# First step of the recurrence's query and forget products in float32, 512-column products in some blocks, and other orders, in a two-layer hybrid block on one Trainium2 core

## The chip, the cores and the metric

The kernel runs on one core of a Trainium2 chip. The metric is the device time of one execution in microseconds; lower is better. In what follows PE is the TensorE matmul unit, PEld its weight load, DVE is VectorE, ACT is ScalarE, POOL is GpSimd, and SP is the SyncE queue that issues most transfers.

## What is computed

The input `x` has 256 tokens of width 1024, one batch, two layers. Shift, scale and gate rows are linear in `silu(c)`, four sets and one for the shared keys and values. Cut to what matters:

```python
h = modulate(x, norm_mix[0], shift, scale)          # layer 0: a gated linear recurrence
q, f, i, g = split(h @ w_in)                        # each 256 x 1024
q = silu(q); log_f = log_sigmoid(f); k = -expm1(log_f)
# per head, chunks of 64 tokens: o = (q * exp(G)) @ state + masked, decayed (q k) @ i
o = rms_norm(o, out_norm) * silu(g)
x = x + gate * (o @ w_out)
x = x + gate * swiglu(modulate(x, ...), ffn_w_in[0], ffn_w_out[0])   # hidden width 2816
kv = modulate(x, kv_norm, ...) @ w_kv               # shared keys, values: compressed, selected, window
q, gates = modulate(x, norm_mix[1], ...) @ w_q      # layer 1: attention, 16 heads of 64, 3 branches
x = x + gate * (attention(q, kv, gates) @ w_out)
x = x + gate * swiglu(modulate(x, ...), ffn_w_in[1], ffn_w_out[1])
```

All inputs and outputs are float32.

## The kernel before

**Products.** Activations lie transposed, feature on the partition, 8 chunks of 128 features by 256 tokens. A float32 product is made of three faster products of split operands: weights are split into `wh` (a rounded copy, type fp32r, made by ACT) and `wl` (the rest, made by DVE), activations into `hh` and `hl`. `mm3` (lines 533 to 537) does `wh·hh`, `wh·hl`, `wl·hh`, 256 columns each. `gemm_wide` (539 to 548) does the first two as one product of 512 columns over `hh` and `hl`, into two halves of a PSUM tile that are added afterwards, and the third with 256 columns. Before, the wide form runs in both second products of the feed-forward layers (`ffo`, from `g`), and in the first product of layer 1 from block 3 on (`WIDE = (1,)`). Small attention products take float32 operands directly, and each shows as two instructions in the trace.

**Weights.** All weights are one list of 1 MB pieces, `SCHED`, in the order in which they are used. SP loads them in that order into a ring of four buffers (`raw`, line 298); a piece is loaded when the piece four before it is no longer read. `process` (302 to 338) takes the next piece: a `lin` piece is split in two halves, `wh` by ACT (line 321) and `wl` by DVE (line 325); an `ada_ss` or `ada_g` piece is reduced against `silu(c)` by two DVE operations (line 390); `pe_ss` and `pe_g` pieces, for four of the sets, go through PE as 32-column float32 products (line 429). The two late pieces of `w1`, for the compressed keys, are loaded into the tile `h0` (`load_late`, line 360).

**Order.** The program is written down in one order, and a planner orders each engine's instructions before the run, by this order, by what is ready and by priorities (`PRI`; a positive number moves earlier, a negative later). At run time each engine works through its list strictly in order. `ORDER` is the order of the recurrence's steps (`hgrn`), of the attention's steps (`nsa`), and the places of the shift, scale and gate pieces in the lists of three stages (`hada`, `f0`, `f1`): a number is the place in the main list before which a piece is put.

**Start.** `startup` and `first_stat` compute the norm of `x`. The recurrence's `q` and `f` (8 steps `hg_qf`, one per 128 features, 16 output tiles in eight PSUM tiles) alternate with the 8 pieces of scale and shift rows of the first set. `first_product` (line 611) does step 0 by hand: the split of its weights in three parts, `t` (L630), `hh` (L631), `hl` (L633), with the order on ACT and DVE written out by `chain`. `first_chunk` makes `hh` and `hl` of the later steps (L745 to L750).

**Tiles.** `h_tiles` gives the activations of two alternating sets: set 0 is one tile `h0` with `hh` and `hl` side by side per chunk, set 1 two tiles `hh1` and `hl1`. The same two tiles hold scratch at the start (`sqs`, `xr0`) and in the recurrence (`s0`, `s1`).

**Attention.** `nsa` computes shared keys and values from the un-normalised `h` where it can (`gemm_deferred`), then two normalised sets by `full_pair`: `hq` for queries and `hk` for values. The masks `QACT` and `KACT` say for which of the 8 chunks ACT makes `t`; DVE makes the others. `hk` takes the tile `h0`, which the late pieces of `w1` hold until the compression has read them. The output projection `nsa_out` runs with `gemm` over `self.O`, and `residual` adds into `x` (L800) and makes the next `hh`, `hl` (L586, L587).

Of the kernel before, what the change touches and what calls it, by code (L numbers as in the profile page):

```python
# [11 lines left out]
F32 = mybir.dt.float32  # L12
F32R = mybir.dt.float32r
# [3 lines left out]
AF = mybir.ActivationFunctionType  # L17
ALU = mybir.AluOpType
# [3 lines left out]
P = 128  # L22
S = 256
D = 1024
KD = 8
FH = 2816
NF = FH // P
CH = 2048
# [4 lines left out]
WIDE = (1,)  # L33
ROOTED = [("ffn_in0", 2, 1), ("ffn_in0", 3, 0), ("kv", 2, 0), ("kv", 4, 0), ("ffn_in1", 2, 1), ("ffn_in1", 3, 0)]
PTS = 3
QACT, KACT = 0x0F, 0xF0
CSTK = 7

PRI = {"gates": -100, "av": 10, "res": 60, "rot": -15, "fh": 60}
# [16 lines left out]
def _ada_g(l):  # L56
# [9 lines left out]
        "D0 k i0 +g0 +i1 +g1 S0/4 x c0 c1 D1 i2 +i3 V0 +g2 +T0 S1/4 +g3 x G0 V1 T1 o0 H o1 G1 o2 o3"  # L66
    ).split(),
    "hada": [1, 1, 2, 2, 3, 3, 4, 4, 7, 7, 8, 8],
    "f0": [7, 7, 8, 8, 9, 13, 15, 16, 16, 16, 21, 21, 22, 23, 25, 26, 28, 29, 31, 32],
    "nsa": (  # L70
        "K q0 c0 c1 G w0 q1 R n0 x0 q3 w1 s0 s1 s2 q2 v0 v1 n1 a s3 a s4 v2 a v3 a x1 s5 s6 v4 v6 s7 a a a a v5 a v7 a a a"
    ).split(),
    "f1": [15, 16, 24, 29],
# [126 lines left out]
class K:  # L200
# [364 lines left out]
    def h_tiles(self, which):  # L565
        if which == 0:

            self.h0 = self.hp.tile([P, KD, 2, 258], F32R, tag="h0", name="h0")
            return self.h0[:, :, 0], self.h0[:, :, 1]
        hh = self.hp.tile([P, KD, 258], F32R, tag=f"hh{which}", name=f"hh{which}")  # L570
        hl = self.hp.tile([P, KD, 258], F32R, tag=f"hl{which}", name=f"hl{which}")
        return hh, hl
# [38 lines left out]
    def first_product(self, hh, hl, pool):  # L611
# [5 lines left out]
        ws = [[self.wp.tile([P, CH // 2], F32R, tag=n, name=f"{n}1_{h}") for n in ("wh", "wl")] for h in range(2)]  # L617
        parts = [(0, 0, 2), (0, 2, 8), (1, 0, 8)]

        def hi(h, a, b):  # L620
            return nc.scalar.copy(ws[h][0][:, a * P:b * P], u[:, h * D + a * P:h * D + b * P])

        def lo(h, a, b):
            s = slice(a * P, b * P)
            return nc.vector.tensor_tensor(ws[h][1][:, s], u[:, h * D + a * P:h * D + b * P],
                                           ws[h][0][:, s].bitcast(F32), op=ALU.subtract)

        t = pool.tile([P, 2, S], F32, tag="X", bufs=XBUFS, name="t0")[:, 0]
        his = [hi(*parts[0])]
        ts = nc.vector.scalar_tensor_tensor(t, self.x[:, 0], A[:, 0:1], self.rstd, op0=ALU.mult, op1=ALU.mult)  # L630
        h = nc.scalar.activation(hh[:, 0, :256], t, AF.Identity, bias=sh[:, 0:1])  # L631
        los = [lo(*parts[0])]
        hls = nc.vector.scalar_tensor_tensor(hl[:, 0, :256], t, sh[:, 0:1], hh[:, 0, :256].bitcast(F32),  # L633
                                             op0=ALU.add, op1=ALU.subtract)
        for p in parts[1:]:
            his.append(hi(*p))
            los.append(lo(*p))
        self.chain(*on_act[:-1], his[0], on_act[-1], h, *his[1:])
        self.chain(on_dve[-1], ts, los[0], hls, los[1], los[2])
        self.hl_prev = los[2]  # L640
        self.issue(self.n_proc + RAW)
        return ws
# [5 lines left out]
    def startup(self, crow):  # L648
# [3 lines left out]
        sq = self.hp.tile([P, KD * 258], F32, tag="hh1", name="sqs")[:, :KD * S].rearrange("p (k s) -> p k s", k=KD)  # L652
# [42 lines left out]
    def first_stat(self):  # L695
# [15 lines left out]
        self.xr0 = self.hp.tile([P, KD * 258], F32, tag="hl1", name="xr0")[:, :KD * S].rearrange("p (k s) -> p k s", k=KD)  # L711
# [108 lines left out]
    def hgrn(self):  # L820
# [3 lines left out]
        with self.tc.tile_pool(name="hg", bufs=1) as gp, self.tc.tile_pool(name="hg2", bufs=2) as g2:  # L824
# [4 lines left out]
            for k in range(KD):  # L829
# [10 lines left out]
                for h, w in enumerate(self.fetch("hg_qf", k, ahead=0) if k else self.first_product(hh, hl, g2)):  # L840
# [7 lines left out]
            s0 = self.hp.tile([P, KD * 258], F32, tag="hh1", name="s0")  # L848
# [893 lines left out]
```

## Time and profile before

| | us |
|---|---|
| three runs | 723.38, 720.93, 723.20 |
| median | 723.2 |
| profiled execution, device time | 723.27 |
| its span, first to last instruction | 721.5 |

| engine or path | what the page says |
|---|---|
| granted PE clock, mean | 0.998 |
| HBM read | 170.48 MB, 238 GB/s over the span |
| `raw` pieces of 1024 KB | 153 issues on SP, median 5.5 us to landing |
| `ffo` products (L547, 512 columns) | 330, 116.0 us busy |
| `ff` products (L535, L536, L537, 256 columns) | 352 each, 98.9 to 99.1 us busy |
| reductions on DVE (L390) | 64, 77.9 us busy |

Matmuls are pipelined: a 256-column split product shows some 0.28 us from start to end, while the next one starts about 0.12 us after it. So busy us of PE summed by line exceed the time that passes. A row of the page gives line, engine, operation, output and inputs, shapes and count, then busy us and mean ns of one, then the engine's idle time just before these instructions and what ended it.

### The profile page before, as it was taken

The page shows a single profiled execution, that of the slowest core. Times are in us where ns is not written, and L with a number is a line of the kernel's source. Part 1 is how long each engine was busy: PE and PEld are TensorE (multiplying, and loading weights), DVE is VectorE, ACT ScalarE, POOL GpSimd, SP SyncE. Part 2 cuts the span into 40 slices and gives each one's busy share as a digit, 9 for nine tenths or more (in the row PEclk, how much of TensorE's full clock was granted, in tenths as well). Part 3 has the DMA queues.
Part 4 walks back from the last instruction along what each step waited for, and adds up shares of the span by engine and source line. Part 5 has one row for each costly group of instructions (what it writes and reads, how often), then busy time and mean ns, then how long its engine had stood idle before and what let it go on. Part 6 is the DMA issues. An engine that isn't in the chain of part 4 may idle for free.

```text
span 721.5 us, 14615 instructions
## 1 busy us (share of the span) xinstructions
PE 710.4 (98%) x5843; PEld 628.2 (87%) x5843; DVE 578.9 (80%) x1177; ACT 418.5 (58%) x825; POOL 12.3 (2%) x29
## 2 busy tenths in 40 slices
PE   8999999999999999999999999999999999999998
PEld 5999788899999999988898896555999888888887
DVE  6997896589998989889598798878779878776651
ACT  5659877567636454544376555559657656564430
POOL 0000000000000000000002020100000000000000
PEclk9999999999999999999999999999999999999999
DMA  9899865734599898888548542674445757556720
GB/s 356 334 367 381 334 255 194 269 126 175 179 343 369 315 347 341 318 304 341 198 148 289 207 151 70 248 281 187 176 175 177 256 204 258 202 197 232 241 81 23
DMA packets 27926, 174.05 MB, mean 241 GB/s; under 512 B 3281, under 2 KB 4689, under 8 KB 8018
## 3 DMA queue, kind: packets, MB, share of 16 engines
q1 hardware_dynamic: 26656, 170.80, 64.3%
q0 software_dynamic: 768, 1.57, 0.8%
q8 instruction: 46, 0.75, 0.4%
q10 hardware_dynamic: 434, 0.74, 0.3%
q14 instruction: 22, 0.18, 0.1%
HBM read 170.48 MB, written 1.05 MB: 238 GB/s over the span
## 4 chain that ended last, share of the span: by engine, by line
PE 80%; DVE 7%; ACT 6%; DMA 4%; issue 2%; SPq 0%; ACTq 0%; DVEq 0%
PE ffo L547 11%; PE ff L535 7%; PE ff L537 7%; PE ff L536 6%; PE ffo L548 5%; PE ff L547 5%; DMA raw<-in_w 3%; PE ff L548 2%; PE po L1616 2%; PE adapsss L429 2%; DVE wl L325 2%; ACT wh L321 2%; PE ptt L1598 2%; PE s L1558 2%; ACT Pt L469 1%
## 5 line engine op out<-in xcount | busy, mean ns | idle before, releaser
L321 ACT CAST wh<-raw 128x1024 fp32r<-128x1024 f32 x199 | 206.8, 1049 | 164.0 <-PE ffo L547 43.8
L325 DVE TENSOR_TENSOR wl<-raw,wh 128x1024 fp32r<-128x1024 f32 x199 | 241.2, 1220 | 71.0 <-ACT wh L321 70.9
L547 PE MATMUL ffo<-g,wh 128*128 128x512 f32 x330 | 116.0, 394 | 0.0
L536 PE MATMUL ff<-hl,wh 128*128 128x256 f32 (+1 forms) x352 | 99.1, 282 | 0.0
L537 PE MATMUL ff<-hh,wl 128*128 128x256 f32 (+1 forms) x352 | 99.1, 282 | 0.0
L535 PE MATMUL ff<-hh,wh 128*128 128x256 f32 (+1 forms) x352 | 98.9, 282 | 0.0
L548 PE MATMUL ffo<-g,wl 128*128 128x256 f32 x330 | 93.0, 282 | 0.0
L390 DVE CUSTOM_DVE_ANT_0 junk<-raw,crep 128x1024 f32<-128x1024 f32 x64 | 77.9, 1217 | 3.1 <-DMA raw<-in_w 3.1
L547 PEld LDWEIGHTS ffo<-g,wh 128*128 128x128 f32 x330 | 62.0, 188 | 14.5
L535 PEld LDWEIGHTS ff<-hh,wh 128*128 128x128 f32 x352 | 66.3, 189 | 0.3 <-ACT hh L586 0.2
L537 PEld LDWEIGHTS ff<-hh,wl 128*128 128x128 f32 x352 | 66.5, 189 | 0.0
L536 PEld LDWEIGHTS ff<-hl,wh 128*128 128x128 f32 x352 | 66.4, 189 | 0.0
L548 PEld LDWEIGHTS ffo<-g,wl 128*128 128x128 f32 x330 | 62.0, 188 | 0.0
L547 PE MATMUL ff<-h,wh 128*128 128x512 f32 x152 | 54.1, 394 | 0.0
L548 PE MATMUL ff<-h,wl 128*128 128x256 f32 x152 | 42.6, 281 | 0.0
L469 ACT ACTIVATE Pt<-Pt,nm 128x128 f32<-128x128 f32 x64 | 28.1, 441 | 16.9 <-DVE nm L1567 16.9
L547 PEld LDWEIGHTS ff<-h,wh 128*128 128x128 f32 x152 | 28.7, 189 | 6.6
L548 PEld LDWEIGHTS ff<-h,wl 128*128 128x128 f32 x152 | 28.7, 189 | 0.0
L800 DVE SCALAR_TENSOR_TENSOR x<-ffo,mod,x 128x256 f32<-128x256 f32 x31 | 14.9, 481 | 16.5 <-PE ffo L548 11.5
L530 ACT CAST g<-fg 128x256 fp32r<-128x256 f32 x44 | 17.8, 404 | 17.4 <-DVE fg L1206 16.3
L1563 DVE CUSTOM_DVE_ANT_0 Pt<-s,cst 128x128 f32<-128x128 f32 (+1 forms) x64 | 18.9, 352 | 2.1 <-PE s L1558 2.0
L1042 DVE TENSOR_TENSOR rf<-rf 128x512 f32<-128x512 f32 x28 | 18.3, 685 | 2.2 <-ACT X L1039 1.0
(497 smaller groups left out, 1755.3 us busy)
## 6 DMA issues: line engine op xcount, KB each, us to landing
raw<-in_w SPq DMA_DIRECT2D x153, 1024.0 KB, 5.5
raw<-in_w SPq DMA_DIRECT2D x11, 512.0 KB, 6.9
w1late<-in_w SPq DMA_DIRECT2D x2, 1024.0 KB, 8.7
x<-in_x SPq DMA_DIRECT2D x2, 512.0 KB, 4.7
usq<-huq POOLq DMA_DIRECT2D x16, 64.0 KB, 2.9
out<-x SPq DMA_DIRECT2D x8, 128.0 KB, 1.9
cst<-in_cst ACTq DMA_DIRECT2D x1, 558.0 KB
usk<-huk POOLq DMA_DIRECT2D x8, 64.0 KB, 5.8
```

What stands on the lines that cost most here:

```text
L321: r = nc.scalar.copy(wh, u)
L325: r = nc.vector.tensor_tensor(wl, u, wh.bitcast(F32), op=ALU.subtract)
L390: r = nc.vector.tensor_tensor_reduce(out=junk, in0=t[:, h * D:(h + 1) * D], in1=self.crep, scale=1.0, scalar=0.0, op0=ALU.mult, op1=ALU.ad ...
L469: r = nc.scalar.activation(out, in_, func, **kw)
L530: self.nc.scalar.copy(hi, v)
L535: mm(ps, lhsT=wh, rhs=hh, start=first, stop=False)
L536: mm(ps, lhsT=wh, rhs=hl, start=False, stop=False)
L537: return mm(ps, lhsT=wl, rhs=hh, start=False, stop=last)
L547: mm(ps, lhsT=w[k][0], rhs=b, start=k == 0, stop=False)
L548: mm(ps[:, 0], lhsT=w[k][1], rhs=b[:, 0], start=False, stop=k == n - 1)
L1042: nc.vector.tensor_tensor(fr, fr, ap(rf, 2 * W, [1, 2], [2, n], [0, b]), op=ALU.mult)
L1563: nc.vector.tensor_tensor_reduce(out=Pt[half][:, br, o:o + n], in0=ps[half][:, br], in1=cs[:, S - n:], scale=1.0, scalar=-3e38, op0=ALU.ad ...
```

## The change

Step 0 of `q` and `f` is no longer split: 16 float32 products run from the loaded weight piece and the float32 activation, for which DVE adds the shift (`tf`). `hh` and `hl` of chunk 0 are still made, for the later products with `h`. Set 1 of the activations becomes one tile `h1`, with all of `hh` before all of `hl`, and so do the scratch tiles in its place. Seven blocks of layer 0's first feed-forward product and the attention's output projection take the wide form; the projection's residual then adds two halves. Orders, places and three masks change.

```diff
-WIDE = (1,)
+WIDE = ((4, 11, 14, 16, 17, 18, 21), range(NF))
-QACT, KACT = 0x0F, 0xF0
+QACT, KACT = 89, 241
+PTV = 1
-PRI = {"gates": -100, "av": 10, "res": 60, "rot": -15, "fh": 60}
+PRI = {'gates': -80, 'av': 10, 'res': 50, 'rot': 0, 'fh': 130}
...
     "hgrn": (
-        "D0 k i0 +g0 +i1 +g1 S0/4 x c0 c1 D1 i2 +i3 V0 +g2 +T0 S1/4 +g3 x G0 V1 T1 o0 H o1 G1 o2 o3"
+        "i0 k +i1 +g0 D0 +g1 S0/4 c0 x i2 c1 V0 +g2 +i3 +T0 D1 S1/4 +g3 x H G0 V1 o0 T1 G1 o1 o2 o3"
...
-    "hada": [1, 1, 2, 2, 3, 3, 4, 4, 7, 7, 8, 8],
-    "f0": [7, 7, 8, 8, 9, 13, 15, 16, 16, 16, 21, 21, 22, 23, 25, 26, 28, 29, 31, 32],
+    "hada": [1, 1, 1, 2, 3, 3, 4, 6, 7, 7, 9, 9],
+    "f0": [5, 6, 7, 8, 9, 10, 12, 13, 15, 19, 20, 20, 22, 23, 26, 26, 26, 27, 30, 32],
     "nsa": (
-        "K q0 c0 c1 G w0 q1 R n0 x0 q3 w1 s0 s1 s2 q2 v0 v1 n1 a s3 a s4 v2 a v3 a x1 s5 s6 v4 v6 s7 a a a a v5 a v7 a a a"
+        "q0 K c1 c0 G w0 q1 R n0 q3 q2 x0 s0 w1 s1 s2 v0 v1 n1 s3 s4 v2 a a v3 a a x1 s5 a s6 v4 v6 s7 v5 a a v7 a a a a a"
...
-    "f1": [15, 16, 24, 29],
+    "f1": [10, 20, 21, 32],
...
-        hh = self.hp.tile([P, KD, 258], F32R, tag=f"hh{which}", name=f"hh{which}")
-        hl = self.hp.tile([P, KD, 258], F32R, tag=f"hl{which}", name=f"hl{which}")
-        return hh, hl
+        self.h1 = self.hp.tile([P, 2, KD, 258], F32R, tag="h1", name="h1").rearrange("p e k s -> p k e s")
+        return self.h1[:, :, 0], self.h1[:, :, 1]
...
-    def first_product(self, hh, hl, pool):
+    def first_product(self, hh, hl, pool, out):
...
-        ws = [[self.wp.tile([P, CH // 2], F32R, tag=n, name=f"{n}1_{h}") for n in ("wh", "wl")] for h in range(2)]
-        parts = [(0, 0, 2), (0, 2, 8), (1, 0, 8)]
...
-        self.chain(*on_act[:-1], his[0], on_act[-1], h, *his[1:])
-        self.chain(on_dve[-1], ts, los[0], hls, los[1], los[2])
-        self.hl_prev = los[2]
+        t = pool.tile([P, 2, S], F32, tag="X", bufs=XBUFS, name="t0")
+        ts = nc.vector.scalar_tensor_tensor(t[:, 0], self.x[:, 0], A[:, 0:1], self.rstd, op0=ALU.mult, op1=ALU.mult)
+        tf = nc.vector.tensor_scalar_add(t[:, 1], t[:, 0], sh[:, 0:1])
+        for h in range(2):
+            for m in range(8):
+                nc.tensor.matmul(out[h][m // 2][:, m % 2], lhsT=u[:, h * D + m * P:h * D + m * P + P], rhs=t[:, 1],
+                                 start=m % 2 == 0, stop=False)
+        self.last_hh = nc.scalar.copy(hh[:, 0, :256], t[:, 1])
+        hls = nc.vector.tensor_tensor(hl[:, 0, :256], t[:, 1], hh[:, 0, :256].bitcast(F32), op=ALU.subtract)
+        self.chain(*on_act, self.last_hh)
+        self.chain(on_dve[-1], ts, tf, hls)
+        self.hl_prev = tf
         self.issue(self.n_proc + RAW)
-        return ws
...
-        sq = self.hp.tile([P, KD * 258], F32, tag="hh1", name="sqs")[:, :KD * S].rearrange("p (k s) -> p k s", k=KD)
+        two = self.hp.tile([P, 2, KD, 258], F32, tag="h1", name="sqs_xr0")
+        sq, self.xr0 = two[:, 0, :, :S], two[:, 1, :, :S]
...
-            s0 = self.hp.tile([P, KD * 258], F32, tag="hh1", name="s0")
-            s1 = self.hp.tile([P, KD * 258], F32, tag="hl1", name="s1")
+            two = self.hp.tile([P, 2, KD * 258], F32, tag="h1", name="s01")
+            s0, s1 = two[:, 0], two[:, 1]
...
-                elif l in WIDE:
+                elif j in WIDE[l]:
+                    both = (self.h1, self.h0)[l]
...
-                        self.gemm_wide(ps[m], self.tiles(ws[m]), lambda k: self.h0[:, k, :, :S])
+                        self.gemm_wide(ps[m], self.tiles(ws[m]), lambda k: both[:, k, :, :S])
...
-                ps = self.acc_tile(f"nso{i}")
                 for m in range(2):
-                    self.gemm(ps[:, m], self.tiles(ws[m]), self.O[0], self.O[1])
-                    self.residual(ps[:, m], 2 * i + m, gate, nxt)
+                    ps = self.acc_tile(f"nso{i}_{m}")
+                    self.gemm_wide(ps, self.tiles(ws[m]), lambda k: self.h0[:, k, :, :S])
+                    self.residual(ps[:, 0], 2 * i + m, gate, nxt, ps[:, 1])
...
-                if half == 0 and br == 0:
+                if PTV >> (2 * br + half) & 1:
                     nc.vector.tensor_copy(d, pt)
```

More of the change, by code (lines that the diff above doesn't have):

```diff
@@ L616, in first_product @@
         self.n_proc += 1
-        ws = [[self.wp.tile([P, CH // 2], F32R, tag=n, name=f"{n}1_{h}") for n in ("wh", "wl")] for h in range(2)]
-        parts = [(0, 0, 2), (0, 2, 8), (1, 0, 8)]
[L620 to L637, printed above, removed]
-        self.chain(*on_act[:-1], his[0], on_act[-1], h, *his[1:])
-        self.chain(on_dve[-1], ts, los[0], hls, los[1], los[2])
-        self.hl_prev = los[2]
+        t = pool.tile([P, 2, S], F32, tag="X", bufs=XBUFS, name="t0")
[10 more added lines that the diff above has]
+        self.hl_prev = tf
         self.issue(self.n_proc + RAW)
-        return ws
     def chain(self, *steps):
@@ L710, in first_stat @@
         self.first_order = on_act + [A, sh], on_dve
-        self.xr0 = self.hp.tile([P, KD * 258], F32, tag="hl1", name="xr0")[:, :KD * S].rearrange("p (k s) -> p k s", k=KD)
     def stat_end(self, ps=None):
@@ L839, in hgrn @@
                     nc.vector.tensor_copy(self.c32, self.cc[:, :, None].to_broadcast([P, 8, 32]))
-                for h, w in enumerate(self.fetch("hg_qf", k, ahead=0) if k else self.first_product(hh, hl, g2)):
+                if k == 0:
+                    self.first_product(hh, hl, g2, (pq, pf))
+                for h, w in enumerate(self.fetch("hg_qf", k, ahead=0) if k else ()):
                     for m, (wh, wl) in enumerate(self.tiles(w)):
```

## The prediction

> **What bounds the kernel now.** I read the page first: busy times, the chain by engine, the two costliest groups.
>
> ```profile
> PE 710.4 (98%) x5843; PEld 628.2 (87%) x5843; DVE 578.9 (80%) x1177; ACT 418.5 (58%) x825; POOL 12.3 (2%) x29
> ...
> PE 80%; DVE 7%; ACT 6%; DMA 4%; issue 2%; SPq 0%; ACTq 0%; DVEq 0%
> ...
> L321 ACT CAST wh<-raw 128x1024 fp32r<-128x1024 f32 x199 | 206.8, 1049 | 164.0 <-PE ffo L547 43.8
> L325 DVE TENSOR_TENSOR wl<-raw,wh 128x1024 fp32r<-128x1024 f32 x199 | 241.2, 1220 | 71.0 <-ACT wh L321 70.9
> ```
>
> TensorE holds the end. Whether that is so in each stage is told by the busy time by stage (columns: stretch, its length, busy us of PE, PEld, DVE, ACT, POOL with counts, clock, DMA share, GB/s).
>
> ```profile
> 75.00:180.00 105.00, 104.81 (x1491) 94.19 (x1490) 83.98 (x186) 75.44 (x152) 0.00 (x0) 1.00 0.62 226
> 180.00:300.00 120.00, 120.00 (x1001) 119.49 (x1000) 110.59 (x197) 62.83 (x100) 0.00 (x0) 1.00 0.84 316
> 300.00:358.00 58.00, 58.00 (x333) 50.73 (x332) 46.93 (x80) 24.37 (x33) 0.00 (x0) 1.00 0.77 284
> 358.00:398.00 40.00, 39.55 (x321) 36.80 (x320) 33.55 (x73) 26.33 (x57) 4.21 (x9) 1.00 0.66 228
> 398.00:405.00 7.00, 5.57 (x31) 5.16 (x32) 6.14 (x12) 4.11 (x11) 0.00 (x0) 0.76 0.74 312
> ...
> 540.00:718.00 178.00, 177.94 (x1060) 157.69 (x1060) 126.41 (x201) 89.09 (x153) 0.00 (x0) 1.00 0.53 189
> ```
>
> From 75 us on PE has hardly a hole except in 398 to 405. So an order can gain little except there and before 75 us; elsewhere only fewer PE cycles help, and an order can lose anywhere. The profiled execution took 723.27 us (span 721.5 plus 1.8 around it); the median of the runs is 723.2, so no correction is needed. The measurement tells a difference of about 0.5%, 3.6 us, from none.
>
> **First step in float32.** Here PE's start hangs on a short chain.
>
> ```profile
> 12.98 0.48 DVE L630 SCALAR_TENSOR_TENSOR t<-x,modA,rstd 128x256 f32<-128x256 f32 x1
> 13.38 0.42 DVE L625 TENSOR_TENSOR wl<-raw,wh 128x256 fp32r<-128x256 f32 x1
> 13.56 0.51 ACT L631 ACTIVATE h<-t,mod 128x256 fp32r<-128x256 f32 x1 [0.66 <-DVE t L630]
> ...
> 14.13 0.58 PE L535 MATMUL q<-h,wh 128*128 128x256 f32 x1
> ```
> ```profile
> 21.17 0.62 PE L535 MATMUL q<-h,wh 128*128 128x256 f32 x3 [0.41 <-ACT h L749]
> ```
> ```profile
> 178.75 0.43 PE rb L728 x2
> ```
> ```profile
> L762 DVE TENSOR_SCALAR t<-xr,modA,mod x4: 405/406/414, 375.9 to 381.2; 128x256 f32<-128x256 f32 x4
> ```
>
> Today 48 split products run from 14.13, and the second step starts at 21.17. After: `t` at 13.46, the new add of the shift like L762, 0.41, so about 13.8, and PE starts near 13.85: 0.3 us earlier. A float32 product of this shape is L728's: two instructions, 0.43 us. 16 x 0.43 = 6.9 us. Early PE is slow (the first product shows 0.58); I estimate that 1.5 us of the stream run at half speed, 0.75 more. It ends near 13.85 + 6.9 + 0.75 = 21.5, so the second step is 0.35 us late. ACT loses three casts and DVE three subtractions, each adding up to two whole halves, 2.1 and 2.4 us; neither is what PE waits for after 21 us alone, so I count nothing for them.
>
> The added wait is the raw piece. Today it is free when its last `wl` is done; then when the last product has read it. SP's row of loads:
>
> ```profile
> 17.02 0.33 SPq L298 DMA_DIRECT2D raw<-in_w  x1
> ```
> ```profile
> 19.65 0.33 SPq L298 DMA_DIRECT2D raw<-in_w  x1
> ```
> ```profile
> 24.22 0.33 SPq L298 DMA_DIRECT2D raw<-in_w  x1
> ```
> ```profile
> DMA to landing us min/median/max: 4.7/7.0/11.4
> ```
> ```profile
> 23.40 1.05 ACT L321 CAST wh<-raw 128x1024 fp32r<-128x1024 f32 x1
> ```
> ```profile
> 27.04 0.52 PE L535 MATMUL q<-h,wh 128*128 128x256 f32 x3
> ```
> ```profile
> 33.41 0.39 PE L535 MATMUL q<-h,wh 128*128 128x256 f32 x1 [0.47 <-ACT h L749]
> ```
> ```profile
> 14.10:20.60 6.50, 6.50 (x49) 6.20 (x48) 6.26 (x9) 3.78 (x6) 0.00 (x0) 1.00 0.97 383
> 21.10:62.70 41.60, 40.77 (x337) 40.37 (x338) 37.43 (x55) 28.32 (x48) 0.00 (x0) 1.00 0.94 361
> ```
>
> The load issued at 17.02 brings the third step's weights (`hg_qf` 2). It moves to about 21.8, and behind it on SP stand the next ones: 19.65's (the fourth step's scale rows) moves to about 22, that of 24.22 is not late any more. DMA runs dry meanwhile. The third step's weights land at 21.8 + 4.7 = 26.5, the cast of 23.40 comes then, 1.05 long, and PE can start at 27.6, not 27.04: 0.55 late. The fourth step's rows land 2.5 us later (1 MB at some 0.42 MB per us), 29.0; two reductions and two `wl` of 1.22 each on DVE put its `hh` near 34.0, not 33.41. Then the ring is full again, and the 0.83 us of holes in 21.1 to 62.7 take up part. I take +0.4 at the end of this stage, between -0.3 (only the earlier start counts) and +4.8 (the load's delay, 21.8 - 17.02, never made good).
>
> **512 columns.** Rate of PE with three 256s (first row), and with a 512 and a 256 (second):
>
> ```profile
> 180.00:230.00 50.00, 50.00 (x422) 50.00 (x421) 48.95 (x89) 28.08 (x50) 0.00 (x0) 1.00 0.79 297
> 560.00:600.00 40.00, 40.00 (x231) 35.03 (x230) 32.48 (x53) 23.23 (x43) 0.00 (x0) 1.00 0.65 233
> ```
> ```profile
> L1198 DVE TENSOR_TENSOR u<-ff,u 128x256 f32<-128x256 f32 x19 | 7.9, 416 | 0.0
> ...
> L1197 ACT COPY u<-ff 128x256 f32<-128x256 f32 x19 | 6.9, 364 | 0.0
> ...
> L800 DVE SCALAR_TENSOR_TENSOR x<-nso,mod,x 128x256 f32<-128x256 f32 x8 | 3.8, 481 | 4.9 <-PE nso L537 4.9
> ```
> ```profile
> ACT wh L321 <- PE ff L536: 20.0, 17, 3.8
> ```
> ```profile
> 534.93 0.30 PEld L535 LDWEIGHTS ff<-hh,wh 128*128 128x128 f32 x2 [0.20 <-ACT hh L586]
> ```
>
> A triple costs 3 x 50/422 = 0.355 us, a pair 2 x 40/231 = 0.346: 0.009 less, though the columns are the same 768. Seven blocks of 16 triples: -1.0; by the median spacing it is nearer 0.7, I take -0.8. Each such block adds two L1197 and two L1198, 0.73 us of ACT and 0.83 of DVE, 5.8 us of DVE in all. DVE has 120 - 110.59 = 9.4 us free in 180 to 300, and casts wait 20 us for PE to free pieces in that stretch: covered, though thinly up to 230 (48.95 of 50). Without cover it is up to +5.8. [...]
>
> The output projection has 64 triples: -0.5. Each of its 8 residuals gets a second L800, 0.48. After the last one the next product's weight load already waits 0.20 for `hh`, so the last addition comes out in full: +0.5. Each column block now takes an `acc` buffer of its own, 2.8 us of PE work each; with three of them two residuals may lag, so no wait is added. Together 0.
>
> **Orders, and chunks by mask.** The new copy mask puts the same single copy on DVE as the old test: 0. `QACT` keeps four chunks on ACT, `KACT` has five for four, 0.2 us moved: 0. The one tile `h1` is released when both halves are: its users end together, 0. The shift and gate loads (`hada`, `f0`, `f1`) keep their number; moved, each costs DVE or PE the same. The last gate load of `f1` goes from before chunk 7 to before chunk 10 of the second product; it gates rows 6 and 7 alone, which end last: 0. The new order of the recurrence works between 75 and 180 us, where PE idles 0.2 us: nothing to gain, and what it might lose stands in the bound below. The priorities `res`, `rot` and `fh` move instructions on ACT and DVE within stages that PE fills: 0. What an order can gain is in these rows:
>
> ```profile
> 398.00:401.00 3.00, 1.57 (x10) 1.16 (x11) 2.20 (x5) 1.99 (x5) 0.00 (x0) 1.00 1.01 423
> 401.00:404.50 3.50, 3.50 (x19) 3.50 (x19) 3.47 (x8) 1.62 (x6) 0.00 (x0) 0.51 0.62 262
> ```
> ```profile
> 400.74 0.39 PE L990 MATMUL v<-wh,h 128*128 128x256 f32 x1 [1.00 <-DVE h L531]
> ```
> ```profile
> 73.80 0.39 PE L537 MATMUL hg_g<-h,wl 128*128 128x256 f32 x1 [0.63 <-DVE wl L325]
> ```
>
> PE idles 1.43 us in 398 to 401, waiting in its fixed order for `h` while gate products are ready, and then runs at half clock: 0.49 x 3.5 = 1.7 us. 3.1 together. `gates` is raised from -100 to -80, and the query comes before `K`; both may put ready products into this hole. I take a third, -1.0, between -3.1 and, with a hole of the same kind elsewhere, +3.1.
>
> Sum: 723.3 + 0.4 - 0.8 + 0 - 1.0 = **721.9 us**.
>
> **Rivals.** (a) The new orders close the holes: -0.4 from the counted edits, -3.1, -0.45 (358 to 398), -0.6 (73.80): 718.7. For it: products ready and only queued behind. Against: the order is fixed before the run, and DMA at 423 GB/s was the late party there. [...]
>
> (b) Slower: the held raw piece empties DMA's ring, and it stays behind. Price: up to 4.8 us, minus 0.8 for the wide blocks: about 727. It decides if loads stay back to back yet PE still waits for weights at the sixth step. For it: a share of 0.94 in 21.1 to 62.7. Against: 361 GB/s there, 423 in 398 to 401, so a seventh is free, 6 us of the 41.6.
>
> (c) Slower: DVE falls behind in 190 to 230, where a shift load now stands before nearly each block from 5 to 10, and block 4 is wide. 5.8 - 0.8: about 728.
>
> (d) The pair isn't cheaper from the new tile, whose halves lie apart rather than side by side: 0.8 back, 722.7, no change either.
>
> **Chances.** Forecast 0.47, (a) 0.32, (b) 0.11, (c) 0.06, (d) 0.04. Faster by over 0.5% (under 719.6): 0.32; within: 0.51; slower: 0.17. The forecast's own range is 719.8 to 724.5. For 8 in 10 the range reaches (a) with some room and part of (b): 717.0 to 726.2.
>
> **What would show it.** 32 float32 instructions from 13.8 to 21.5, and the sixth load of weights issued near 21.8 in place of 17.02; the third step near 27.6; a start stage ending within 0.6 us of today's; seven blocks 0.1 us shorter with no PE wait on `wl`; the clock whole or halved near 400. Wrong if the third step starts later than 29, if DVE's `wl` ends PE's waits in 190 to 230, or if a new PE hole of over 2 us stands behind 62 us.

## The result and the profile after

The changed kernel takes **716.68 us**, median of four runs (715.79 to 717.07), beside 722.38 for four runs of the kernel before (720.93 to 723.38). The ratio is 0.9924, 95% interval [0.9912, 0.9937]. Predicted were 721.9 us with a range of 717.0 to 726.2: faster than forecast by 5.2 us, and 0.3 us under the range. The profiled execution took 716.88 us, its span 715.1.

From the page of the changed kernel, the busy times and the chain by engine:

```profile
PE 704.2 (98%) x5651; PEld 616.5 (86%) x5651; DVE 583.6 (82%) x1196; ACT 421.7 (59%) x837; POOL 12.3 (2%) x29
...
PE 89%; DVE 4%; DMA 4%; ACT 2%; issue 1%; SPq 0%; DVEq 0%; ACTq 0%
```

PE still holds the end, by 89% of the chain instead of 80%. It has 192 products fewer and is busy 6.2 us less, about what the span lost. That suggests that the gain is PE's own time, but it doesn't say in which stage, and a wait or a half clock can be counted as busy, too (both turn up below). For this I lay the first PE product of each stage, read from the timelines of the two profiled executions, side by side. Lengths between these marks in us; `q`, `hg_i`, `ff` and so on are the tiles that the products write:

| from the first product of ... to that of ... | before | changed | difference | predicted |
|---|---|---|---|---|
| q, hg_i: the recurrence's q and f | 48.51 | 47.93 | -0.6 | +0.4 |
| hg_i, ff: the recurrence | 104.03 | 103.28 | -0.75 | 0 |
| ff, ffo: first feed-forward, in | 129.49 | 128.84 | -0.65 | -0.8 |
| ffo, k: its out, keys and values | 74.94 | 74.85 | -0.1 | 0 |
| k, gates | 26.73 | 26.39 | -0.35 | 0 |
| gates, kcms: the hole near 400 | 12.32 | 10.43 | -1.9 | -1.0 |
| kcms, nso: attention | 96.93 | 96.54 | -0.4 | 0 |
| nso, ffo: output projection, second feed-forward, in | 148.95 | 147.31 | -1.65 | 0 |
| ffo, last instruction | 65.42 | 65.42 | 0 | 0 |

The differences sum to -6.4, as the two profiled times do (723.27 and 716.88). Of the terms that weren't 0, only the wide blocks came out as predicted. Five stages that were put down as 0 gave 3.2 us together, the start had the wrong sign, and the stretch with the hole gave nearly twice its share.

The hole itself is still there. The changed kernel's rows (stretch, its length, busy us of PE, PEld, DVE, ACT and POOL with counts, clock, DMA share, GB/s) and its PE timeline:

```profile
398.00:405.00 7.00, 7.00 (x60) 6.99 (x60) 6.60 (x18) 5.12 (x13) 0.00 (x0) 1.00 0.42 174
...
394.68:398.09 3.41, 2.41 (x17) 1.66 (x14) 2.16 (x5) 2.23 (x5) 0.00 (x0) 1.00 1.01 406
```
```profile
397.88 0.39 PE L979 MATMUL v<-wh,h 128*128 128x256 f32 x1 [1.00 <-DVE h L532]
```

398 to 405 is now full and at full clock, since everything comes 2.4 us earlier: the hole lies in 394.68 to 398.09, PE busy 2.41 of 3.41 us. The same product waits the same 1.00 us for the same `h`. What went is the half clock behind it, not the hole.

### The profile page after: what moved, and what is told of

Same layout as the page of the kernel before. It is cut to its first block, busy times and chain, and to the rows that moved or that the text cites. A ratio compares the mean times of both kernels' runs of the same rounds, so it can differ in the third digit from the quotient of the medians.

```text
span 715.1 us, 14268 instructions
## 1 busy us (share of the span) xinstructions
PE 704.2 (98%) x5651; PEld 616.5 (86%) x5651; DVE 583.6 (82%) x1196; ACT 421.7 (59%) x837; POOL 12.3 (2%) x29
## 4 chain that ended last, share of the span: by engine, by line
PE 89%; DVE 4%; DMA 4%; ACT 2%; issue 1%; SPq 0%; DVEq 0%; ACTq 0%
PE ffo L548 11%; PE ff L548 7%; PE ffo L549 5%; PE ff L537 5%; PE ff L538 5%; PE ff L536 5%; DMA raw<-in_w 4%; PE ff L549 3%; PE po L1606 2%; PE s L1548 2%; PE adapsss L430 2%; PE nso L548 2%; PE ptt L1588 2%; PE hg_g L536 1%; PE hg_i L977 1%; PE adapsg L430 1%
## 5 line engine op out<-in xcount | busy, mean ns | idle before, releaser
L538 PE MATMUL ff<-h,wl 128*128 128x256 f32 (+1 forms) x288 | 81.1, 282 | 0.0
L537 PE MATMUL ff<-h,wh 128*128 128x256 f32 (+1 forms) x288 | 81.0, 282 | 0.0
L536 PE MATMUL ff<-h,wh 128*128 128x256 f32 (+1 forms) x288 | 80.9, 282 | 0.0
L548 PE MATMUL ff<-h,wh 128*128 128x512 f32 x208 | 74.0, 394 | 0.0
L549 PE MATMUL ff<-h,wl 128*128 128x256 f32 x208 | 58.4, 281 | 0.0
L536 PEld LDWEIGHTS ff<-h,wh 128*128 128x128 f32 x288 | 54.2, 189 | 0.3
L538 PEld LDWEIGHTS ff<-h,wl 128*128 128x128 f32 x288 | 54.4, 189 | 0.0
L537 PEld LDWEIGHTS ff<-h,wh 128*128 128x128 f32 x288 | 54.3, 189 | 0.0
L548 PEld LDWEIGHTS ff<-h,wh 128*128 128x128 f32 x208 | 39.2, 189 | 8.8
L549 PEld LDWEIGHTS ff<-h,wl 128*128 128x128 f32 x208 | 39.2, 188 | 0.0
L548 PE MATMUL nso<-h,wh 128*128 128x512 f32 x64 | 22.4, 394 | 0.0
```

Of the source, the lines that this page charges most:

```text
L536: mm(ps, lhsT=wh, rhs=hh, start=first, stop=False)
L537: mm(ps, lhsT=wh, rhs=hl, start=False, stop=False)
L538: return mm(ps, lhsT=wl, rhs=hh, start=False, stop=last)
L548: mm(ps, lhsT=w[k][0], rhs=b, start=k == 0, stop=False)
L549: mm(ps[:, 0], lhsT=w[k][1], rhs=b[:, 0], start=False, stop=k == n - 1)
```

## The experiments

All are timed against the kernel before on the same chip; in 95 runs beside them it had a median of 721.6 us. "Stage" numbers are lengths between the marks of the table above, from one profiled execution each. The three profiled executions of the changed kernel tell how far such numbers scatter: by 1.15 us from hg_i to ff, by 0.4 to 0.5 from gates to kcms and from kcms to nso, by 0.2 or less in the other stages.

### Each part alone

**e1_first**: only the float32 first step.

```diff
-                for h, w in enumerate(self.fetch("hg_qf", k, ahead=0) if k else self.first_product(hh, hl, g2)):
+                if k == 0:
+                    self.first_product(hh, hl, g2, (pq, pf))
+                for h, w in enumerate(self.fetch("hg_qf", k, ahead=0) if k else ()):
```

> Only the float32 first step is taken over. Theory A (each edit brings its own PE time, and they add): the start stage, up to the first value product, ends 0.6 us earlier than before, 62.0 in place of 62.6, and the whole is 0.6 us faster. Theory B (the new orders bring the gain): no change within 0.3 us. The recorded prediction's step would have +0.4 us. If the third step's weights are issued near 17 us, the held weight piece does not delay them; near 21.8 it does.

719.9 us (10 runs), ratio 0.998 [0.997, 0.9989]. Its start takes 47.89 us, as in the changed kernel. The part alone is worth 0.6 us there, and is no loss. The other 1.0 us of its time lies from gates to kcms (9.56 us, against 10.6 in the kernel before without the half clock), which the last group takes up.

**e2_nso**: only the output projection in 512 columns.

```diff
-                ps = self.acc_tile(f"nso{i}")
                 for m in range(2):
-                    self.gemm(ps[:, m], self.tiles(ws[m]), self.O[0], self.O[1])
+                    ps = self.acc_tile(f"nso{i}_{m}")
+                    self.gemm_wide(ps, self.tiles(ws[m]), lambda k: self.h0[:, k, :, :S])
```

> Only the wide output projection is taken over. Theory A: the stretch from the first product of the projection to the first product of the second feed-forward half takes 1.6 us less than before's 148.95, and the whole is 1.6 us faster. Theory B: 0 to -0.3 us, the rest of that stretch's gain belongs to the orders. The recorded prediction's step: 0 (0.5 won by fewer weight loads, 0.5 lost by the second addition).

719.79 us (10 runs), ratio 0.9985 [0.9973, 0.9997]; the stage from nso to ffo 147.25 us, -1.70, the whole difference seen in the changed kernel.

**e2_last**: as e2_nso, but the last of the four column pairs stays in three products with one addition.

```diff
+                    if i < 3:
                         self.gemm_wide(ps, self.tiles(ws[m]), lambda k: self.h0[:, k, :, :S])
+                    else:
+                        self.gemm(ps[:, 0], self.tiles(ws[m]), self.O[0], self.O[1])
```

> The kernel before with the wide output projection in its first three of four column pairs, the last pair as three products of 256 columns with one addition each. Theory A (the second addition of the last column block costs nothing at the hand-over, since products of the next stage stand ready): the stretch from the first product of nso to the last rb loses a quarter of its gain, 31.12 becomes 31.4 to 31.7 us, the time 720.1. Theory B (as predicted, the last addition costs its full 0.48 us): 30.9 us in that stretch, 719.6.

719.7 us (8 runs), ratio 0.9971 [0.9961, 0.9981]. The last `rb`, the product that spreads the norm's factor, was a poor mark: it comes 29.9 us after the first nso, in e2_nso 31.1, but more of the next stage is left then. To the first ffo the two stand at 147.38 and 147.25. A quarter of the pairs' gain is 0.31 us (worked out below), and the stage is 0.13 longer, so leaving out the last second addition gives back 0.2 us at most, not 0.48. That lies between the two theories, nearer to A.

**e3_wide0**: only the joint tile and the seven wide blocks, old orders.

```diff
-WIDE = (1,)
+WIDE = ((4, 11, 14, 16, 17, 18, 21), range(NF))
```

> Only the seven wide blocks of layer 0 and the one tile they need are taken over, with the old places of the shift and gate pieces. Theory A: the first product of layer 0's feed-forward takes 0.65 to 0.8 us less than before's 129.5 and the whole is that much faster. Theory B: the wide blocks need the new places as cover on DVE; with the old places DVE falls behind, PE waits for wl and the stage is 1 us or more longer.

722.62 us (10 runs), ratio 1.0013 [0.9997, 1.0028]. The blocks do bring their 0.64 us from ff to ffo (128.85), and the whole shows nothing of it. Part of that is the clock: five of these ten runs have a mean clock of 0.997 or 0.998, the mark of a half-clocked stretch (next group), against 14 of the 95 of the kernel before. Where the rest went is the question of the last group.

**e4_orders**: only orders, priorities and masks.

```diff
-PRI = {"gates": -100, "av": 10, "res": 60, "rot": -15, "fh": 60}
+PRI = {'gates': -80, 'av': 10, 'res': 50, 'rot': 0, 'fh': 130}
...
-        "D0 k i0 +g0 +i1 +g1 S0/4 x c0 c1 D1 i2 +i3 V0 +g2 +T0 S1/4 +g3 x G0 V1 T1 o0 H o1 G1 o2 o3"
+        "i0 k +i1 +g0 D0 +g1 S0/4 c0 x i2 c1 V0 +g2 +i3 +T0 D1 S1/4 +g3 x H G0 V1 o0 T1 G1 o1 o2 o3"
```

> Only the orders, places, priorities and masks are taken over; all products as before. Theory A: 1.5 us or less faster where the clock stays full near 400 us in both kernels' runs, and some 1.7 us more in runs where before's clock halves there and this one's doesn't. Theory B: 4 us faster or more, most of the change's 5.7.

719.85 us (10 runs), ratio 0.9976 [0.9962, 0.999]; the recurrence 102.32 us, -1.7. Its start, with the old first step, takes 47.96 us, as short as the changed kernel's 47.93.

Beside 721.5 us of the kernel before, the four parts alone differ by -1.6, -1.7, +1.1 and -1.7 us, -4.0 together; the whole change (716.6 us over 14 runs, below) by about -5. Each of the four carries an interval of 0.7 to 1.1 us either way, so these times can't tell whether the parts add.

**o_rec**: of the orders, only `hgrn` and `hada`. **o_nsa**: only `nsa` and the priorities. Their diffs are these lines of the change, alone.

> The kernel before with only the new order of the recurrence and its gate loads. Theory A (fewer changes between wide and narrow products on TensorE, each near 0.2 us there and back, and no wait for the second half of the first output gate's weights): the stretch from the first product of hg_i to the first of ff falls from 104.0 to 102.3 us, and the time by 1.7 us, to about 719.6. Theory B (TensorE was full there, so the gain of the orders kernel came from its priorities or its later orders): 104.0 us in that stretch and a time of 721.3.

> The kernel before with only the new order of the attention stage and the new priorities. Theory A (this order brings 0.7 us from the query's products to nso, the recurrence's order the rest of the orders' gain): from the first product of k to the first of nso without a fallen clock 133.5 us instead of 134.3, and a time near 720.7, with the clock falling near 400 us in as many runs as before (8 of 48). Theory B (the gain of the whole orders kernel came from here): 719.8.

o_rec: 720.85 us (12 runs), ratio 0.9988 [0.9976, 1.0001], with 102.34 us from hg_i to ff. The stage gain is the recurrence's order and nothing else: all seven profiled executions with the old order have 103.7 to 104.3 us there (mean 104.0), all thirteen with the new one 102.0 to 103.4 (mean 102.6; f_gates and the kernels of the last group included). The time is 0.6 us shorter, with an interval that reaches from 1.7 us to nothing. In the profiled execution a late load in the start and a half-clocked window hide the gain; why the median of twelve runs doesn't show more of it stays open. o_nsa: 721.2 us (12 runs), ratio 0.9996 [0.9985, 1.0007]: no difference that can be measured, and 2 of its 12 runs have a mean clock of 0.998.

How does an order gain 1.7 us where PE is "busy"? The whole stretch, first in the kernel before, then in o_rec:

```profile
62.64:166.67 104.03, 103.21 (x1537) 90.25 (x1535) 80.41 (x170) 77.26 (x151) 0.00 (x0) 1.00 0.68 248
```
```profile
64.04:166.38 102.34, 102.26 (x1536) 90.14 (x1535) 80.47 (x170) 77.74 (x151) 0.00 (x0) 1.00 0.68 251
```

0.74 of the 1.69 us was idle time, mostly the wait for `wl` at 73.80 that the prediction quoted. 0.95 us was counted as busy. Summed from each product's start to the next one's, the 64 products of `adapsss` (the gate and scale rows, 32 columns wide in the array) take 8.53 us before and 7.55 in o_rec, though the products are the same. The excess lies in 16 of them, which run among `psu` products from 131.00 us on in the kernel before: 2.95 us, where 16 in one block take 1.86. So PE waited there, too, while the profile, which models the ends of products, showed it busy; what it waited for isn't shown. The reason that theory A gave, fewer changes between wide and narrow products, isn't borne out: there are 48 changes between products 128 and 32 columns wide in both (a change there and back does cost some 0.2 us: in the kernel before 0.21 and 0.22 us pass from start to start at 77.32 and 77.91, instead of 0.12). Its number for the stage was right, its time of 719.6 didn't show, and its waits were right in part.

### The hole and the clock

**a_again** and **a_again_2**: the changed kernel unchanged, ten more runs.

> The changed kernel once more, beside the kernel before, to see how far both scatter and how often the clock falls to one half near 400 us. Theory A (the fall comes when a 3.41 us window of the clock holds a product stream that is busy for less than about half of it; the hole near 396 us is the same in both kernels and only its place in the window differs from run to run): most runs near 716.7 us, and some near 718.4 with a mean clock of 0.998. Theory B (the changed orders removed the fall): no run above 717.5.

> The changed kernel a third time, beside the next one, to tell whether it is slower than without the seven wide blocks. Theory A (the blocks' 0.65 us is given back): 716.2 to 716.7, a first values' load that is cast 10.0 to 10.6 us after its issue. Theory B (chance): the same time as the next kernel plus or minus 0.2.

716.37 us (5 runs), ratio 0.993 [0.9913, 0.9948]; the second time 717.1, ratio 0.993 [0.9916, 0.9944]. No run had a mean clock of 0.998, which is for theory B, but with few runs. e4_orders has one such run of ten, so the orders alone don't remove the fall.

The kernel before settles more. In its profiled execution the clock is 0.50 in one window of 3.41 us (401.07 to 404.48), which costs half of that, 1.7 us, and the mean clock is 0.998. Of its 95 runs 14 have that mean clock (median 723.3 us), 81 have not (721.4). The execution that the prediction was worked out on was one of this kind. Which runs are hit seems to hang on where the clock's windows fall; I count them in steps of 3.41 us from the changes of the clock in each trace (last section). Before's window with the hole, and o_rec's, both followed by half clock:

```profile
397.66:401.07 3.41, 1.98 (x14) 1.39 (x11) 2.27 (x5) 2.34 (x5) 0.00 (x0) 1.00 1.01 423
401.07:404.48 3.41, 3.41 (x18) 3.41 (x17) 3.38 (x7) 1.53 (x5) 0.00 (x0) 0.50 0.61 257
```
```profile
397.19:400.60 3.41, 1.93 (x13) 1.20 (x12) 2.06 (x4) 2.13 (x5) 0.00 (x0) 1.00 1.01 425
```

And those of e2_nso and of u_first (below), after which the clock stayed whole:

```profile
397.66:401.08 3.42, 2.15 (x15) 1.60 (x13) 2.48 (x6) 2.37 (x6) 0.00 (x0) 1.00 1.02 429
```
```profile
395.66:399.07 3.41, 1.93 (x14) 1.72 (x15) 3.22 (x8) 2.36 (x8) 0.00 (x0) 1.00 1.02 430
```

The same hole stands in all four: 1.27 to 1.48 us of idle time by these rows, in the kernel before in two pieces of 0.43 and 1.00. Near 400 us the clock fell behind windows in which PE was busy 1.83 to 1.98 us (the third is o_nsa's), 54 to 58% of them and not under half as theory A has it, and not behind those with 2.07 and more. So how much of the hole one window catches seems to matter. It isn't the whole rule: u_first's 1.93 didn't halve the clock, with weight loads (the next number) at 1.72 us instead of 1.2 to 1.4, and two windows elsewhere fall on the wrong side. The first, f_gates' (below), was followed by half clock; the second, o_rec's, was not:

```profile
441.40:444.81 3.41, 2.50 (x10) 1.09 (x8) 3.09 (x24) 3.41 (x17) 0.00 (x0) 1.00 0.02 5
444.81:448.23 3.42, 3.42 (x11) 1.87 (x10) 3.42 (x16) 3.35 (x16) 0.00 (x0) 0.50 0.00 0
```
```profile
38.79:42.20 3.41, 1.78 (x15) 1.58 (x14) 3.33 (x4) 2.17 (x5) 0.00 (x0) 1.00 0.94 384
```

What exactly decides stays open.

**f_gates**: the changed kernel with the ready gate products put ahead.

```diff
-PRI = {'gates': -80, 'av': 10, 'res': 50, 'rot': 0, 'fh': 130}
+PRI = {'gates': 300, 'av': 10, 'res': 50, 'rot': 0, 'fh': 130}
```

> The changed kernel with the gate products put ahead of the last compression products (one priority, -80 to 300). Theory A (TensorE's hole of 1.4 us near 396 us is a wait for the value product's first weights while ready products stand behind it): about 2 us of gate products and compression products fill it, the time falls by 1.4 us to about 715.3, and no run has its clock halved there. Theory B (the wait moves: the compression's tail or the values' weights come later by as much): 716.7 us, with a hole of over 1 us somewhere from 396 to 412.

725.51 us (7 runs), ratio 1.0054 [1.0034, 1.0074], **slower** by 9 us than the changed kernel. Theory A fell, and B was too mild. PE's waits on its timeline:

```profile
400.18 0.39 PE L979 MATMUL v<-wh,h 128*128 128x256 f32 x1 [0.83 <-DVE h L532]
408.56 0.44 PE L1458 MATMUL hidt<-cst,hid 128*128 128x128 f32 x2 [1.96 <-DVE hid L1450]
```

The compression ends later, so its tail is now waited for (1.96 us). The attention behind it, from s to nso, takes 74.4 us instead of 65.8, with a half-clocked window in it. I didn't follow that stage further.

### Where the wide blocks' gain goes

**u_wide0** (three times, 13 runs): the changed kernel without the seven blocks. **u_h1**: also without the joint tile.

```diff
-WIDE = ((4, 11, 14, 16, 17, 18, 21), range(NF))
+WIDE = ((), range(NF))
```

> The changed kernel without the seven wide blocks of the first feed-forward (the joint tile stays). Theory A (they bring their products' difference, 0.65 us, also under the new order of gate loads): 0.65 us slower, 717.3. Theory B (they bring nothing to the whole, as when they stood alone on the kernel before, 722.6 against 721.5): 716.7 or less.

> The changed kernel without the seven wide blocks once more, now for its time. Theory A (the blocks gain 0.65 us in their stage and lose as much or more by meeting a later load near 396 us): 715.3 to 716.4, not above the changed kernel's 716.4 to 716.7. Theory B (the first time was chance): 717.0 to 717.4.

> The changed kernel without the seven wide blocks, a third time. Theory A: 0.4 to 0.7 us under the changed kernel, 715.8, the values' load cast 8.9 to 9.5 us after its issue. Theory B: within 0.2 us of it, or above.

> The changed kernel without the seven wide blocks and without the joint tile, which nothing else needs. Theory A (the joint tile costs nothing, since the users of its halves end together): the time of the kernel that keeps the tile, 715.8. Theory B (work waits for the other half of the tile, in the recurrence where xr and the scan's slots share it): 0.3 to 1.0 us faster, 715.0, with the stretch from the first hg_i to the first ff under 102.0 us.

715.79, 716.15 and 716.01 us, ratios 0.9917 [0.99, 0.9934], 0.9917 [0.9901, 0.9932], 0.9916 [0.9901, 0.9932]; u_h1 716.28, ratio 0.9919 [0.9905, 0.9933]. All 13 runs have a median of 715.94, the changed kernel's 14 runs one of 716.6: the blocks save 0.65 us in their stage and bring nothing, rather a loss (on the same chip 715.79 beside 716.37, and 716.01 beside 717.1). The joint tile does nothing that shows: u_h1's recurrence of 102.4 us lies among the 102.0 to 103.4 of u_wide0's three profiled executions, which keep the tile.

**f_w**: the kernel before with the float32 step, the joint tile and the seven blocks. **u_first**: the changed kernel with the old first step. Both are put together from the parts above.

> The kernel before with the float32 first step, the joint tile and the seven wide blocks, and its old orders. Theory A (the wide blocks shift the loads against TensorE, so that the values' load near 388 us comes later by the time that they saved): gates to kcms 10.4 to 10.8 us, against 9.56 with the float32 step alone, and a time of 719.7 to 720.3, no better than with the float32 step alone (719.9). Theory B (the later load has nothing to do with them): gates to kcms near 9.6 and a time of 719.3.

> The changed kernel with the old first step of 48 split products. Theory A (the float32 step brings 0.6 us at the end of the start, and keeps it): from the first product of q to the first of hg_i 48.0 to 49.8 us instead of 47.9 to 48.1, and 717.3 us. Theory B (as predicted, the float32 step costs 0.4 us there): 716.0.

f_w: 720.41 us (11 runs), ratio 0.9986 [0.9977, 0.9995], and 11.04 us from gates to kcms instead of 9.56 in e1_first. u_first: 716.75 us (5 runs), ratio 0.9935 [0.9918, 0.9953], its start 47.96 us. Theory A's 717.3 and B's 716.0 both missed: inside the whole change the first step's gain can't be told from none, as the new orders alone shorten the start as much (e4_orders).

What stands in that stretch is a transfer. The load of the values' weights goes out on SP, and ACT casts it when it lands. The plan puts the activations `h` that PE waits for behind this cast on ACT and behind its `wl` on DVE, and the traces show them in that order. In the changed kernel ACT casts at 394.85, then come:

```profile
395.80 0.71 ACT L531 CAST h<-t 128x256 fp32r<-128x256 f32 x2
```
```profile
395.93 1.23 DVE L326 TENSOR_TENSOR wl<-raw,wh 128x1024 fp32r<-128x1024 f32 x1 [4.79 <-ACT wh L322]
...
397.41 0.75 DVE L532 TENSOR_TENSOR h<-t,h 128x256 fp32r<-128x256 f32 x2
```

PE goes on at 397.88. In all kernels one load of instructions (a packet of 16 KB, 1.07 us long in the changed kernel, 1.09 in the kernel before) goes by near this place. f_gates has another order there; in the 19 other profiled executions, those of w8 and w6 below included, the stretch from gates to kcms takes 10.4 to 11.0 us (without the half clock) wherever the instructions start 5.5 to 7.8 us after the issue of the values' load (13 of them), and 9.2 to 9.7 where they start at 8.1 or later (6). ACT's cast compares only within one order of the attention: 9.25 to 9.7 against 8.1 us after the issue with the old one, 10.1 to 10.7 against 8.9 to 9.4 with the new one. Some of them (before, f_w and e1_first have the old order):

| kernel | instruction load starts, us after the load's issue | ACT's cast, us after it | gates to kcms |
|---|---|---|---|
| before | 6.8 | 9.42 | 12.32, of it 1.7 the clock's |
| changed | 7.2 | 10.13 | 10.43 |
| u_first | 6.9 | 10.74 | 10.99 |
| f_w | 6.2 | 9.68 | 11.04 |
| e1_first | 9.3 | 8.10 | 9.56 |
| u_wide0_2 | 8.3 | 8.88 | 9.20 |
| u_h1 | 9.8 | 9.09 | 9.39 |

In the kernel before the packet falls inside, the first step alone moves it past, and the seven blocks move the packet ahead of it into its place (from 376.1 us in e1_first to 393.4 in f_w). That fits if these are PE's instructions, loaded as it uses them up: fewer products ahead move them later. This is my inference, as the trace names the queue `instruction` and no engine. The counts fit it, too: the kernel before has 46 packets for 5843 products and as many weight loads, the changed one 44 for 5651, some 254 and 257 instructions to a packet, while DVE and ACT have more instructions in the changed kernel, not fewer. Two kernels test that.

**w8**: eight wide blocks. **w6**: six.

```diff
-WIDE = ((4, 11, 14, 16, 17, 18, 21), range(NF))
+WIDE = ((4, 11, 14, 16, 17, 18, 20, 21), range(NF))
```

> The changed kernel with an eighth wide block (20) in the first feed-forward: 32 TensorE instructions fewer ahead of the attention stage, of 64 bytes each by estimate (a block of instructions of 16384 bytes comes about every 15 us, while TensorE issues some 256). Theory A (a load of instructions of 16 KB, 1.07 us long on one of the DMA engines, falls into the values' load when it starts 10.8 to 12.2 us after the first w1late load, and past it when it starts later): it starts about 2 us later than in the changed kernel, at 13 us or more, the stretch from gates to kcms falls from 10.4 to 10.8 us to under 9.8, and the time to 715.4. Theory B (the wide blocks themselves make the load late, the more the later): 10.8 to 11.0 us in that stretch, 716.6.

> The changed kernel with six wide blocks (21 left out): 32 TensorE instructions more. Theory A: the load of instructions starts about 2 us earlier, at 9 to 10 us after the first w1late load, still while loads stand in the queue, so the stretch from gates to kcms stays at 10.4 to 10.8 us, and the time at 716.7. Theory B (each wide block makes the load a seventh of 1.2 us later): 10.4 us or less in that stretch, 716.5.

w8: **715.1 us** (5 runs, 714.85 to 715.78), ratio 0.9907 [0.9893, 0.9922], 9.21 us from gates to kcms. w6: 716.87 us (6 runs), ratio 0.9931 [0.9918, 0.9943], 10.48 us. B falls: the eighth block brings 1.2 us in that stretch, where B has it lose. A's stretch and time came true, but not its condition: the instruction load came 0.9 us later against the first w1late load, at 12.0 us, inside the 10.8 to 12.2 that A had called harmful. Against the issue of the values' load it starts at 8.1 us, just past the latest harmful one (7.8, e4_orders). So the dividing line was drawn after these runs, and it is narrow. The changed kernel's SP, ACT and DMA views, the last for 391.9 to 393.0 us:

```profile
384.72 8.63 SPq L299 DMA_DIRECT2D raw<-in_w  x4
```
```profile
394.85 1.05 ACT L322 CAST wh<-raw 128x1024 fp32r<-128x1024 f32 x1 [5.37 <-DMA raw<-in_w]
```
```profile
q8 instruction: 1, 0.02, 6.1%
```

And w8's, the last for 392.4 to 393.6 us:

```profile
384.41 8.13 SPq L299 DMA_DIRECT2D raw<-in_w  x4
```
```profile
393.32 1.05 ACT L322 CAST wh<-raw 128x1024 fp32r<-128x1024 f32 x1 [4.16 <-DMA raw<-in_w]
```
```profile
q8 instruction: 1, 0.02, 5.5%
```

With the same issue time within 0.3 us, ACT casts at 394.85 in the one and at 393.32 in the other. In w8 the packet of instructions starts 0.8 us before the cast, when little of the load is left. PE's timeline of w8 shows no wait in 394 to 400. w8 has the lowest median of all; each of its runs is under each of the changed kernel's 14, the closest by 0.01 us.

## Why the prediction was wrong, step by step

**The start of the sum.** 723.3 us, "so no correction is needed": that step failed. The profiled execution had a half-clocked window, whose mean clock 14 of 95 runs have, and two of the three runs shown lie at its time. The others take 721.4. Of the 6.4 us between the two profiled executions 1.7 are this and no work of the change. As a change, -1.4 us was forecast and about -5 came: of the miss of 5.2 us some 1.7 are the start of the sum, and 3.5 lie in the steps that follow.

**First step, +0.4: no loss, -0.6 alone.** The failed step is "the piece four before": I let SP's load at 17.02 wait until PE is done with the first piece, near 21.8. In the changed kernel's SP and PE timelines:

```profile
17.39 5.05 SPq L299 DMA_DIRECT2D raw<-in_w  x3
```
```profile
14.11 3.72 PE L622 MATMUL q<-t,raw 128*128 128x256 f32 x16 [0.60 <-DVE t L619]
17.67 3.62 PE L622 MATMUL f<-t,raw 128*128 128x256 f32 x16
20.93 0.82 PE L536 MATMUL q<-h,wh 128*128 128x256 f32 x4
```

The load goes out at 17.39, into the buffer of the second piece of scale rows, which DVE had read by 17.36. The ring's buffers needn't come free in the order of their loads. The buffer that PE holds goes to the next load, which waits until 21.32 instead of 19.65, for PE's last product at 21.29, and costs nothing that shows. The duration was right (20.93 - 14.11 = 6.82 us for 16 products, 0.426 each); the 0.75 us for half speed, an estimate from before's first product, weren't paid, as the clock was whole from 12.39 in that execution (in the kernel before from 15.36, its products taking 0.58 us at 14.13 and 0.28 from 15.42 on). But the -0.6 of the start isn't the step's alone: with the old step and the new orders it is as short (47.96 us in e4_orders and in u_first). With the old step six other profiled executions have 48.5 to 50.1 us there, all twelve with the new step 47.7 to 48.2. Rival (b) with it is out: DMA moved more, not less, in the same stretch as before's:

```profile
21.10:62.70 41.60, 40.99 (x342) 40.65 (x340) 37.47 (x55) 27.37 (x47) 0.00 (x0) 1.00 0.97 373
```

**Seven wide blocks, -0.8: right in their stage (-0.65), wrong for the whole.** DVE covers the additions, as 180 to 300 shows: PE is without a hole and DVE has 6.45 us free. So rivals (c) and (d) are out.

```profile
180.00:300.00 120.00, 120.00 (x888) 114.31 (x888) 113.55 (x208) 66.68 (x112) 0.00 (x0) 1.00 0.85 316
```

The step that was missing is what the saved time meets later: as far as the last group shows it, the 112 products fewer bring a load of instructions into the values' load, which costs the 1.2 us that w8 gets back.

**Output projection, 0: wrong, -1.65.** Two terms failed. "-0.5": the triples' price came from another stage. Here, first and last starts by line, first of the kernel before, then of e2_nso:

```profile
L535 PE MATMUL nso<-h,wh x64: 276/280/387, 507.1 to 533.0; 128*128 128x256 f32 x64
```
```profile
L547 PE MATMUL nso<-h,wh x64: 389/393/476, 505.4 to 527.5; 128*128 128x512 f32 x64
L548 PE MATMUL nso<-h,wl x64: 276/280/286, 505.7 to 527.7; 128*128 128x256 f32 x64
```

Start to next start, before's 64 triples take 23.65 us (0.369 each, against 0.355 in 180 to 230), since a block's first products often come late; the pairs take 22.40, 0.350 each. That is -1.24. "+0.5, the last addition comes out in full": it didn't, the rest of the stage is 0.45 us shorter. The 0.20 us wait of the weight load that I built on is gone, and so are two others, of 0.20 and 0.15 us, on DVE's residuals. That these make up the 0.45 isn't shown.

**Orders.** "PE idles 0.2 us: nothing to gain" failed: the recurrence's order gives 1.7 us in its stage (o_rec; 1.4 on the mean of all profiled executions), of which the changed kernel's shows 0.75, as PE stalled once for 0.91 us in it (last section). The stretches k to gates and kcms to nso, put down as 0, gave another 0.7 in that execution; in the other two of the changed kernel the second of them is as long as before. "A third of the hole": right that something near 400 us goes, wrong in what. PE's order there is the same before and after (five gate products, two of v, one of nq, then the wait), so neither the raised `gates` nor the query did anything there. Of the 1.9 us there 1.7 are the clock's, and most runs of the kernel before don't lose them either.

**What it would show.** Held: 32 float32 instructions from 14.1 on, a start within 0.6 us, no PE wait on `wl` in 190 to 230, a clock that is whole near 400, and no new hole of over 2 us. Not held: the load near 21.8, and the third step near 27.6 (it starts at 26.86). Rival (a), 718.7, was nearest, and its side, faster by over 0.5%, had been given 0.32. But its mechanism held only in the wait at 73.80 us (0.63), which the new order closes; the hole near 400 us stayed.

## What to carry to other kernels

Before a sum is made on one profiled execution, look whether that execution is a usual one: one half-clocked window was a quarter of the difference between the two profiles here. A stage in which PE is "busy" 99% needn't be full (of the 1.69 us that o_rec won in one, 0.95 had been counted as busy): sum from start to start, and take a product's price from the stage in which it is changed. A gain in one stage counts only if the next transfer that PE waits for comes earlier, too (the seven blocks' 0.65 us brought the whole nothing); where it doesn't, look at what passes on the DMA queues beside it, loads of instructions included.

## What was not expected of the hardware

**The clock's windows.** In the profiled execution of the kernel before the clock is whole from 15.36 us, falls to 0.50 at 401.07 and is whole again at 404.48: 113 steps of 3.413 us lie between the first two changes, one between the last two. In the changed kernel it is whole from 12.39, 2.97 us earlier, which is no whole step, so the steps lie elsewhere in that execution. In the kernel before a window with PE busy 1.98 of 3.41 us was followed by one at 0.50, with no gap over 1.00 us in it.

**Loads of instructions.** 44 packets of 16 KB pass in the changed kernel beside the weights (queue, packets, MB, share of the engines' time):

```profile
q8 instruction: 44, 0.72, 0.4%
```

One of them, 1.07 us long, seems to make a load of 1 MB over 1 us late (from its issue to the cast 10.13 us, in w8 8.91), so that one wide block more, some 100 us earlier, decides 1.2 us. PE seems to starve for them as well: in the changed kernel's recurrence it stops among small products with nothing to wait for, 1.6 us behind the start of such a packet (129.35 to 130.40). Of the thirteen profiled executions with the new order of the recurrence, the eight in which this packet starts 66.8 us or more after the first product of hg_i all stop there, for 0.23 to 0.91 us; the five in which it starts at 66.4 or before don't stop. That PE's list has run out in these moments is argued from this, not shown.

```profile
130.70 0.25 PE L1108 MATMUL psu<-s 128*32 128x64 f32 x2
131.86 0.19 PE L1112 MATMUL psu<-X 128*32 128x32 f32 x1 [0.91 <-issue]
```

Open remains whether a pad of instructions alone would do what the eighth block does: it wasn't tried.
